# ConvFFN up-projection: the RMSNorm's token factor on the activations instead of on the products

## The chip, the cores and the metric

The kernel runs on one core of a Trainium2 chip. The metric is the device time of one execution in microseconds (us). The core's engines are named as in the profile: PE is TensorE (matmuls; PEld its weight loads), DVE is VectorE, ACT is ScalarE, POOL is GpSimd, and SP (SyncE) issues the weight DMAs. Each engine works off its own queue in order and waits there for the results of the others.

## The reference

Two layers act on x of shape (1, 512, 1024), in float32. Each has a mixer (retention and a state-space scan in layer 0; a convolution module and a complex-diagonal S5 in layer 1), and then a gated ConvFFN, which the change is about:

```python
def rms_norm(x, g, eps=EPS):
    xf = x.astype(F32)
    y = xf * lax.rsqrt(jnp.mean(xf * xf, axis=-1, keepdims=True) + eps)
    return (y * g.astype(F32)).astype(x.dtype)

def conv_ffn(h, w_up, dw_w, dw_b, w_down):
    a = causal_dwconv(h @ w_up, dw_w, dw_b)
    gate, up = jnp.split(a, 2, axis=-1)
    return (jax.nn.silu(gate) * up) @ w_down
...
        f = conv_ffn(rms_norm(x, ffn_norm[i]), ffn_w_up[i], ffn_dw_w[i], ffn_dw_b[i], ffn_w_down[i])
        x = x + f.astype(x.dtype)
```

`w_up` is 1024 x 5632, `w_down` 2816 x 1024. The norm's factor is one number for each token, so it can be applied to the activations ahead of `h @ w_up`, or to the product after it.

## The kernel before

**Tiles.** Channels lie on the 128 partitions and the 512 tokens along the free axis. `x` is eight tiles 128x512. A product in float32 is formed from three matmuls on parts with fewer bits: weights and activations are split into a high part and the rest (`whi`, `wlo`; `xh`, `xl`), and `mm3` adds whi*xh, whi*xl and wlo*xh in PSUM. One *column tile* of the up-projection is 8 channel chunks x 3 = 24 matmuls of 128x512 into one PSUM tile `pup` (four of them). Its weights come by DMA into `wraw` (4 buffers); ACT forms `whi` and DVE `wlo` (3 buffers each, `wload`).

**The norm.** `norm_chunk` splits x*g, without the token factor, into `xh` and `xl` while the layer before still ends. The factor row `R` (128x512, the same on all partitions) is ready only after `norm_end`, which runs behind the first column tile. So `ffn` multiplies each product by `R` when it leaves PSUM (`ffh`, DVE).

**The loop.** `ffn` runs over 22 steps i. Each makes two column tiles, j = i (gate) and j = 22 + i (up); the text numbers these tiles n0 to n43 in the order in which they run. Each tile goes through `ffh` (DVE), the first tap with bias on ACT (`ffa`) and two more taps on DVE (`ffa`, SCALAR_TENSOR_TENSOR). Then ACT's SiLU and DVE's product give `ffg`, which is split into `acth` (ACT) and `actl` (DVE), kept for the down-projection (`pdn`).

**Beside it.** In layer 0, each step takes one piece of a generator, `s5_prep`, which forms the S5 parameters of layer 1. `weights(q)` makes, for four q, `w1r`, `w1i` in six products on POOL (with the scratch `s5t`) and `w2r`, `w2i` in six on DVE (with `s5u`). `store(q)` writes `w2d` and `w1d` by DMAs from POOL; for `w1d`, PE transposes `w1` into PSUM (`pw`) and ACT copies that into `s5t` and `s5u`; four pairs of short matmuls give `pG`. POOL also issues DMAs of a zero tile (`tpd`). Layer 1's ConvFFN has no such work.

**Order.** A scheduler places the instructions of all engines when the program is built, by its own estimates of their times; the order in which an engine's instructions stand is fixed from then on. The code gives only the dependences, the buffers and the order of writing. An instruction added in one place can so move others on every engine.

Of the kernel before, what the change touches and what calls it, by code (L numbers as in the profile page):

```python
# [9 lines left out]
F32 = mybir.dt.float32  # L10
F32R = mybir.dt.float32r
I32 = mybir.dt.int32
AF = mybir.ActivationFunctionType
ALU = mybir.AluOpType
# [5 lines left out]
KC = D // P  # L20
# [5 lines left out]
NPAIR = SH // 2  # L26
POOLTAPS = {0: range(1, 31), 3: range(11, 31)}
WV0 = (0, 1, 3, 6)
PACK0 = (("g_mix0", KC),)
PACK1 = (("ident", P), ("tri", P), ("cw", 48), ("cb", 12), ("dtb", SH), ("alog", SH), ("dsk", NPAIR),  # L30
         ("snw", NPAIR))
# [4 lines left out]
class Trunk:  # L36
    def __init__(self, ctx, tc, ins):
# [14 lines left out]
        self.c = {}  # L52
        self.unpack("c0", PACK0, nc.scalar)
        self.onec = self.const.tile([P, 1], F32, name="onec")
# [1 line left out]
        nc.scalar.activation(self.small("warm", [P, 1], 1), self.onec, AF.Square)  # L56
        self.x = [self.xp.tile([P, T], F32, name=f"x{c}") for c in range(KC)]

    # ---------------------------------------------------------------- helpers
    def unpack(self, name, items, eng):  # L60
        t = self.const.tile([P, sum(n for _, n in items)], F32, name=name)
        eng.dma_start(t, self.ins[name])
        at = 0
        for k, n in items:
            self.c[k] = t[:, at:at + n]
            at += n
# [87 lines left out]
    def norm_chunk(self, st, c, stat=True):  # L154
# [8 lines left out]
        if stat:  # L163
            self.stat_add(st, x)

    def norm_end(self, st):
        st["col"] = self.rstd_cols(st["acc"], D, "rs")
        st["R"] = self.rows(st["col"])

    # ---------------------------------------------------------------- ConvFFN  # L170
    def ffn(self, l, st, nxt, aside=None, out=None):
        nc = self.nc
        ins = self.ins
        dw, db = self.dw[l], self.db[l]
        act = []
        for i in range(NFF):
            ab = []
            for j in (i, NFF + i):
                p = self.pp("pup")
                self.proj(p, ins[f"wup{l}"][j], st["h"])  # L180
                if i == 0 and j == 0:
                    self.norm_end(st)
                h = self.tmp("ffh")
                nc.vector.tensor_tensor(h, p, st["R"], op=ALU.mult)  # L184
                a = self.tmp("ffa")
                nc.scalar.activation(a, h, AF.Identity, scale=dw[:, j, 2:3], bias=db[:, j:j + 1])  # L186
                for tap in (1, 0):
                    s = 2 - tap
                    nc.vector.scalar_tensor_tensor(a[:, s:], h[:, :T - s], dw[:, j, tap:tap + 1], a[:, s:],  # L189
                                                   op0=ALU.mult, op1=ALU.add)  # L190
                ab.append(a)
            if aside is not None:
                next(aside, None)
            gs = self.tmp("ffg")
            nc.scalar.activation(gs, ab[0], AF.Silu)
            nc.vector.tensor_tensor(gs, gs, ab[1], op=ALU.mult)  # L196
            hi, lo = self.slot("acth", F32R), self.slot("actl", F32R)
            self.split(gs, hi, lo)
            act.append((hi, lo))
        nst = self.norm_begin(nxt)  # L200
        spans = [slice(k, min(k + 8, NFF)) for k in range(0, NFF, 8)]
        wdn = lambda c, s: ins[f"wdn{l}"][c, :, s.start * P:s.stop * P]
        for c in range(KC if out is None else KC - 1):
            p = self.pp("pdn")
            for s in spans:
                self.proj(p, wdn(c, s), act[s], start=s.start == 0, stop=s.stop == NFF)
            nc.vector.tensor_tensor(self.x[c], self.x[c], p, op=ALU.add)
            if out is None:
                self.norm_chunk(nst, c)
            else:  # L210
                self.stat_add(nst, self.x[c])
                self.gain(nst, c, slice(0, T))
        if out is None:
            return nst
        # the last channels by halves of the tokens, so that the first half leaves under the second
        c = KC - 1
        w = [self.wload(wdn(c, s), (s.stop - s.start) * P) for s in spans]
        HT = T // 2
        for t in range(2):
            ts = slice(t * HT, (t + 1) * HT)  # L220
            p = self.pp("pdn")[:, :HT]
            for i, s in enumerate(spans):
                self.proj(p, None, [(h[:, ts], lo[:, ts]) for h, lo in act[s]], start=i == 0,
                          stop=s.stop == NFF, w=w[i])
                if t and i == 0:
                    self.finish(nst, 0, out)
            nc.vector.tensor_tensor(self.x[c][:, ts], self.x[c][:, ts], p, op=ALU.add)
        self.finish(nst, 1, out)
# [43 lines left out]
    def load_x(self):  # L272
# [3 lines left out]
        for c in range(KC):  # L276
            nc.sync.dma_start(self.x[c], self.ins["xT"][c])
            self.norm_chunk(st, c, False)
            if c in WV0:
                n = min([k for k in (*WV0, KC) if k > c]) - c  # L280
                hi, lo = self.wload(self.ins["wv0"][:, c * 272:(c + n) * 272], n * 272)
# [3 lines left out]
                self.ident = self.c["ident"]  # L285
        return st

    # ---------------------------------------------------------------- even mixer
    def even(self, st):
        nc = self.nc  # L290
        ins = self.ins
# [7 lines left out]
        def cproj(j, w=None):  # L299
            p = self.pp("pxbc")  # L300
            self.proj(p, ins["wxbc"][j], xs, w=w)
            return p

        # values of the first head and dt, tokens on the partitions
        mm = nc.tensor.matmul
        pv = [self.ps("pv0") for _ in range(NT)]
        for k in range(KC):
            hi, lo = st["w"][k]
# [8 lines left out]
        xd, e, z, z2, q, dt, dA, acs, dec, cdl = [sm("dt" + str(i)) for i in range(10)]  # L317
# [4 lines left out]
        first = [cproj(8), cproj(10)]  # L322
# [2 lines left out]
        self.norm_end(st)  # L325
        R, col = st["R"], st["col"]

        # dt
        bc = lambda t: t.unsqueeze(1).to_broadcast(CH)
        for t in range(NT):  # L330
            nc.vector.scalar_tensor_tensor(xd[:, t, :], xd[:, t, :], col[:, t:t + 1], dtb, op0=ALU.mult, op1=ALU.add)
# [16 lines left out]
        p = self.ps("pacs")  # L348
# [6 lines left out]
        p = self.ps("pacsT")  # L355
# [114 lines left out]
                self.split(y, hi, lo)  # L470
                mix[8 + pr] = (hi, lo)

        # retention
        cosR, sinR = self.slot("cosR"), self.slot("sinR")
        with self.tc.issue_after(self.dma_mark.ins):
            nc.gpsimd.dma_start(cosR, ins["cosT"])
# [131 lines left out]
        self.add_mark = s5_mark  # L608
        return nst

    # ---------------------------------------------------------------- S5 parameters
    def s5_prep(self):
        nc = self.nc
        ins = self.ins
# [5 lines left out]
        def sm(shape=S16):  # L620
            n_[0] += 1
            return self.s5p.tile(shape, F32, name=f"s5_{n_[0]}")
# [6 lines left out]
        with self.tc.issue_after(self.dma_mark.ins), self.tc.issue_after(self.add_mark.ins):  # L629
            lr, li, ls = ld("s5ar", S16), ld("s5ai", S16), ld("s5ls", S16)  # L630
            half = lambda: [t for s_ in [self.slot("s5m")] for t in
                            (s_[:, :256].rearrange("p (a c) -> p a c", c=16),
                             s_[:, 256:].rearrange("p (a c) -> p a c", c=16))]
# [3 lines left out]
            step, x, th, k, m1, m8, s, c, si, co = [sm() for _ in range(10)]  # L637
            magic = 12582912.0
            t, t2_, xc, kk = [sm() for _ in range(4)]
# [38 lines left out]
            den, fr, fi, e = [sm() for _ in range(4)]  # L678
# [22 lines left out]
            def cmul(o_r, o_i, ar, ai, xr, xi, t):  # L701
                tt(o_r, ar, xr, op=ALU.mult)
                tt(t, ai, xi, op=ALU.mult)
                tt(o_r, o_r, t, op=ALU.subtract)
                tt(o_i, ar, xi, op=ALU.mult)
                tt(t, ai, xr, op=ALU.mult)
                tt(o_i, o_i, t, op=ALU.add)
# [7 lines left out]
            S256 = [P, 16, 16]  # L715
            b = lambda t: t.unsqueeze(2).to_broadcast(S256)
            cmul(bbr, bbi, b(fr), b(fi), br, bi, bt)
            # powers by descending exponent: qr[., j] = a^(7-j); the same for a^(8-j)
            pw2_ = self.slot("s5p2")
            qr, qi, wr, wi = [pw2_[:, P * i:P * i + P].rearrange("p (a m) -> p a m", m=8) for i in range(4)]  # L720
            for j in range(8):
# [7 lines left out]
            self.rotd = self.dram.tile([3, 2, P, T], F32, name="rotd")  # L729
            zt = self.slot("s5z")  # L730
            eng.memset(zt, 0.0)
            # chunk rotation e^(i 8 theta k) and the decay |a|^8
            cur = (co, si)
            for n in range(3):
                nx = (sm(), sm())
# [77 lines left out]
            yield  # L813
        toep()

    # ---------------------------------------------------------------- odd mixer
    def odd(self, st):
        nc = self.nc
        ins = self.ins
# [238 lines left out]
        return nst  # L1058


# ---------------------------------------------------------------- host layout
def wtiles(w):
    k, m = w.shape
    return w.reshape(k // P, P, m // P, P).transpose(2, 1, 0, 3).reshape(m // P, P, k)
# [20 lines left out]
def layout(i):  # L1085
# [42 lines left out]
    o["s5dd"] = dd.reshape(P, 512)  # L1128
    for name, items in (("c0", PACK0), ("c1", PACK1), ("c2", PACK2)):
        o[name] = np.concatenate([c[k].reshape(P, -1) for k, _ in items], axis=1)  # L1130
# [28 lines left out]
```

## Time and profile before

| | us |
|---|---|
| median of 3 runs | 1400.68 (1399.62 to 1402.01) |
| span of the profiled execution | 1400.0 |
| PE busy | 1331.6 (95%) |
| DVE busy | 991.1 (71%) |
| ACT busy | 547.9 (39%) |
| POOL busy | 299.2 (21%) |
| up-projection of layer 0 | 412.3 to 678.7 |
| up-projection of layer 1 | 1025.2 to 1266.2 |

The profile takes one execution; all times in rows are us from its start. The span ends 0.7 below the median of the runs. In a row of the timeline, the first number is the start, the second the duration, and a bracket holds the idle time of the engine before it and what ended it. Successive instructions of an engine overlap a little (an end counts the last write), so the cost of one in a full queue is the distance of two starts.

### The profile page before, as it was taken

How to read it: one execution, taken by the hardware profiler on the slowest of the kernel's cores; microseconds unless marked ns; L12 is line 12 of the kernel's file. 1: busy time of each engine (PE TensorE's matmuls, PEld its weight loads, DVE VectorE, ACT ScalarE, POOL GpSimd, SP SyncE). 2: the span in 40 equal slices, each digit the busy share in tenths (PEclk: the TensorE clock that was granted, in tenths of full speed). 3: DMA queues.
4: the chain of work that ended last, by engine and by line, in shares of the span. 5: the costliest groups of instructions: out<-in, count | busy, mean ns of one | idle time of the engine just before them, and what ended most of it. 6: DMA issues, size and time to landing. Idle time of an engine off the chain costs nothing.

```text
span 1400.0 us, 17171 instructions
## 1 busy us (share of the span) xinstructions
PE 1331.6 (95%) x6468; PEld 1104.2 (79%) x6468; DVE 991.1 (71%) x1573; ACT 547.9 (39%) x769; POOL 299.2 (21%) x420
## 2 busy tenths in 40 slices
PE   8999999999999899999999987968799999999997
PEld 7788888888887778888888865756588888888887
DVE  6887777688578998777533369999887777774333
ACT  5455444444353334444322221143444444443221
POOL 0210010002009446800000059769000000000100
PEclk9999999999999999999999997888899999999999
DMA  6432232231244434532333332401142333232321
GB/s 218 153 121 69 75 113 91 90 105 64 90 142 121 124 95 139 177 106 87 98 98 94 106 113 83 143 16 53 62 134 94 103 91 106 90 97 88 102 75 61
DMA packets 48803, 143.00 MB, mean 102 GB/s; under 512 B 6352, under 2 KB 7680, under 8 KB 48720
## 3 DMA queue, kind: packets, MB, share of 16 engines
q1 hardware_dynamic: 42560, 124.34, 28.0%
q0 software_dynamic: 5872, 17.37, 4.3%
q8 instruction: 51, 0.84, 0.2%
q14 instruction: 32, 0.26, 0.1%
q10 hardware_dynamic: 288, 0.19, 0.0%
HBM read 131.88 MB, written 9.99 MB: 101 GB/s over the span
## 4 chain that ended last, share of the span: by engine, by line
PE 78%; DVE 17%; issue 2%; POOL 2%; ACT 1%; DMA 0%; DVEq 0%; ACTq 0%; POOLq 0%
PE pup L101 10%; PE pup L99 10%; PE pup L100 10%; PE pdn L101 6%; PE pdn L99 6%; PE pdn L100 6%; DVE cv L861 3%; DVE wlo L90 3%; PE po L99 2%; PE po L101 2%; PE po L100 2%; DVE ffa L189 1%; PE pxbc L100 1%; PE pxbc L99 1%; PE pxbc L101 1%
## 5 line engine op out<-in xcount | busy, mean ns | idle before, releaser
L89 ACT CAST whi<-wraw 128x1024 fp32r<-128x1024 f32 (+3 forms) x246 | 231.0, 940 | 492.5 <-PE pup L100 131.5
L90 DVE TENSOR_TENSOR wlo<-wraw,whi 128x1024 fp32r<-128x1024 f32 (+3 forms) x242 | 272.7, 1128 | 137.6 <-ACT whi L89 137.5
L101 PE MATMUL pup<-xh,wlo 128*128 128x512 f32 x704 | 276.1, 392 | 9.0 <-DVE wlo L90 9.0
L99 PE MATMUL pup<-xh,whi 128*128 128x512 f32 x704 | 276.5, 393 | 0.0
L100 PE MATMUL pup<-xl,whi 128*128 128x512 f32 x704 | 275.2, 391 | 0.0
L101 PEld LDWEIGHTS pup<-xh,wlo 128*128 128x128 f32 x704 | 133.1, 189 | 38.2 <-DVE wlo L90 10.1
L100 PEld LDWEIGHTS pup<-xl,whi 128*128 128x128 f32 x704 | 133.2, 189 | 27.7
L99 PEld LDWEIGHTS pup<-xh,whi 128*128 128x128 f32 x704 | 133.2, 189 | 27.3
L189 DVE SCALAR_TENSOR_TENSOR ffa<-ffh,c,ffa 128x511 f32<-128x511 f32 (+1 forms) x176 | 149.8, 852 | 2.9
L99 PE MATMUL pdn<-acth,whi 128*128 128x512 f32 (+1 forms) x374 | 140.9, 377 | 0.0
L100 PE MATMUL pdn<-actl,whi 128*128 128x512 f32 (+1 forms) x374 | 140.8, 377 | 0.0
L101 PE MATMUL pdn<-acth,wlo 128*128 128x512 f32 (+1 forms) x374 | 140.8, 377 | 0.0
L184 DVE TENSOR_TENSOR ffh<-pup,R 128x512 f32<-128x512 f32 x88 | 60.5, 687 | 63.6 <-PE pup L101 63.3
L231 POOL TENSOR_SCALAR x<-x,c 128x512 f32<-128x512 f32 (+1 forms) x9 | 9.3, 1034 | 402.0 <-ACT acc L127 302.9
L186 ACT ACTIVATE ffa<-ffh,c 128x512 f32<-128x512 f32 x88 | 71.9, 817 | 49.5 <-DVE ffh L184 47.3
L100 PEld LDWEIGHTS pdn<-actl,whi 128*128 128x128 f32 x374 | 70.4, 188 | 12.9
L101 PEld LDWEIGHTS pdn<-acth,wlo 128*128 128x128 f32 x374 | 70.4, 188 | 12.9
L99 PEld LDWEIGHTS pdn<-acth,whi 128*128 128x128 f32 x374 | 70.4, 188 | 12.8
L100 PE MATMUL po<-ml,whi 128*128 128x512 f32 x192 | 76.5, 399 | 3.8 <-DVE ml L95 3.8
L99 PE MATMUL po<-mh,whi 128*128 128x512 f32 x192 | 76.2, 400 | 0.5 <-ACT mh L94 0.5
L101 PE MATMUL po<-mh,wlo 128*128 128x512 f32 x192 | 76.3, 397 | 0.1
L94 ACT CAST acth<-ffg 128x512 fp32r<-128x512 f32 x44 | 27.3, 621 | 106.7 <-DVE ffg L196 104.4
(424 smaller groups left out, 2436.3 us busy)
## 6 DMA issues: line engine op xcount, KB each, us to landing
wraw<-in_wup_dram SPq DMA_DIRECT2D x88, 512.0 KB, 3.5
wraw<-in_wdn_dram SPq DMA_DIRECT2D x32, 512.0 KB, 3.5
wraw<-in_weo_dram SPq DMA_DIRECT2D x32, 256.0 KB, 3.0
wraw<-in_wxbc_dram SPq DMA_DIRECT2D x12, 512.0 KB, 3.7
wraw<-in_wdn_dram SPq DMA_DIRECT2D x16, 384.0 KB, 3.1
wraw<-in_wz_dram SPq DMA_DIRECT2D x8, 512.0 KB, 3.4
wraw<-in_wg_dram SPq DMA_DIRECT2D x8, 512.0 KB, 3.7
ar<-acd POOLq DMA_DIRECT2D x16, 256.0 KB, 4.0
```

The costliest lines, as they stand in the source:

```text
L89: nc.scalar.copy(hi[:, :n], raw[:, :n])
L90: (eng or nc.vector).tensor_tensor(lo[:, :n], raw[:, :n], hi[:, :n].bitcast(F32), op=ALU.subtract)
L94: self.nc.scalar.copy(hi, src)
L99: mm(out, lhsT=w[0], rhs=x[0], start=start, stop=False)
L100: mm(out, lhsT=w[0], rhs=x[1], start=False, stop=False)
L101: self.mark = mm(out, lhsT=w[1], rhs=x[0], start=False, stop=stop)
L184: nc.vector.tensor_tensor(h, p, st["R"], op=ALU.mult)
L186: nc.scalar.activation(a, h, AF.Identity, scale=dw[:, j, 2:3], bias=db[:, j:j + 1])
L189: nc.vector.scalar_tensor_tensor(a[:, s:], h[:, :T - s], dw[:, j, tap:tap + 1], a[:, s:], op0=ALU.mult, op1=ALU.add)
L231: self.nc.gpsimd.tensor_scalar(self.x[c][:, ts], self.x[c][:, ts], st["g"][:, c:c + 1], 1.0, op0=ALU.mult, op1=ALU.mult)
L861: nc.vector.scalar_tensor_tensor(a[:, s:], cin[i][:, :T - s], kw[:, i, 30 - s:31 - s], a[:, s:], op0=ALU.mult, op1=ALU.add)
```

## The change

`PRE` is 3. In the steps i = 0 and 1, after the aside piece, a new `norm_apply` forms for four channel chunks each `xn` = x*R (DVE), `nh` = its high part with the gain g (ACT) and `nl` = the rest (DVE), into 16 tiles of the pool `slot`, in addition to `xh` and `xl`. From i = 3 on (tiles n6 to n43) the matmuls take `nh`, `nl`; there `ffh` falls away, and ACT's tap and the two DVE taps read PSUM. Tiles n0 to n5 stay as they are. It holds for both layers. (In the diff as written, some comments are dropped too; not shown. Line numbers of the changed kernel are larger: `wlo` L91, matmuls L100 to L102, `xn` L171, `nh` L174, `nl` L175, `ffh` L197, taps L201 and L204, S5 products on POOL L720 to L725, on DVE L791 to L796.)

```diff
+PRE = 3
...
+    def norm_apply(self, st, c):
+        nc = self.nc
+        t = self.tmp("xn")
+        nc.vector.tensor_tensor(t, self.x[c], st["R"], op=ALU.mult)
+        hi, lo = self.slot("nh", F32R), self.slot("nl", F32R)
+        g = st["g"][:, c:c + 1]
+        nc.scalar.activation(hi, t, AF.Copy, scale=g)
+        nc.vector.scalar_tensor_tensor(lo, t, g, hi.bitcast(F32), op0=ALU.mult, op1=ALU.subtract)
+        st.setdefault("hn", []).append((hi, lo))
...
                 p = self.pp("pup")
-                self.proj(p, ins[f"wup{l}"][j], st["h"])
+                self.proj(p, ins[f"wup{l}"][j], st["h"] if i < PRE else st["hn"])
                 if i == 0 and j == 0:
                     self.norm_end(st)
-                h = self.tmp("ffh")
-                nc.vector.tensor_tensor(h, p, st["R"], op=ALU.mult)
+                if i < PRE:
+                    h = self.tmp("ffh")
+                    nc.vector.tensor_tensor(h, p, st["R"], op=ALU.mult)
+                else:
+                    h = p
...
             if aside is not None:
                 next(aside, None)
+            if i < PRE - 1:
+                for c in range(i * KC // (PRE - 1), (i + 1) * KC // (PRE - 1)):
+                    self.norm_apply(st, c)
```

The order moves in both ConvFFNs only. First, DVE in layer 0, before: from the first tap of n0 to the `wlo` of tile n5 (`wlo_4325`); `wlo_4288` is n4's.

```order
L189 SCALAR_TENSOR_TENSOR ffa_3905<-ffh_3903,c2_447,ffa_3905 128x511
L90 TENSOR_TENSOR wlo_4288<-wraw_4286,whi_4287 128x1024
L189 SCALAR_TENSOR_TENSOR ffa_3905<-ffh_3903,c2_447,ffa_3905 128x510
L189 SCALAR_TENSOR_TENSOR ffa_3942<-ffh_3940,c2_447,ffa_3942 128x511
L189 SCALAR_TENSOR_TENSOR ffa_3942<-ffh_3940,c2_447,ffa_3942 128x510
L196 TENSOR_TENSOR ffg_4179<-ffg_4179,ffa_3942 128x512
L184 TENSOR_TENSOR ffh_4217<-pup_4186,R_3901 128x512
L90 TENSOR_TENSOR wlo_4325<-wraw_4323,whi_4324 128x1024
```

After, the same stretch has 39 rows. Its last twelve, up to the `wlo` of n5, which is now `wlo_4373`:

```order
L796 TENSOR_TENSOR w2i_4287<-w2i_4287,s5u_4289 128x512
L171 TENSOR_TENSOR xn_4308<-x5_92,R_3901 128x512
L175 SCALAR_TENSOR_TENSOR nl_4305<-xn_4302,c2_447,nh_4304 128x512
L171 TENSOR_TENSOR xn_4314<-x6_93,R_3901 128x512
L175 SCALAR_TENSOR_TENSOR nl_4311<-xn_4308,c2_447,nh_4310 128x512
L171 TENSOR_TENSOR xn_4320<-x7_94,R_3901 128x512
L175 SCALAR_TENSOR_TENSOR nl_4317<-xn_4314,c2_447,nh_4316 128x512
L214 TENSOR_TENSOR ffg_4326<-ffg_4326,ffa_4280 128x512
L175 SCALAR_TENSOR_TENSOR nl_4323<-xn_4320,c2_447,nh_4322 128x512
L197 TENSOR_TENSOR ffh_4364<-pup_4333,R_3901 128x512
L96 TENSOR_TENSOR actl_4330<-ffg_4326,acth_4329 128x512
L91 TENSOR_TENSOR wlo_4373<-wraw_4371,whi_4372 128x1024
```

Between n4's `wlo` and n5's there stood five instructions; now there are 28, among them seven of the eight `nl`, four `xn`, and the six S5 products `w2` of `weights(0)`, which stood behind n5's `wlo` before.

Second, PE in layer 0 at tile n5, before: each tile is 24 matmuls in a row.

```order
L99 MATMUL pup_4322<-xh_3569,whi_4324 128x512
L100 MATMUL pup_4322<-xl_3570,whi_4324 128x512
L101 MATMUL pup_4322<-xh_3569,wlo_4325 128x512
L99 MATMUL pup_4322<-xh_3595,whi_4324 128x512
L100 MATMUL pup_4322<-xl_3596,whi_4324 128x512
L101 MATMUL pup_4322<-xh_3595,wlo_4325 128x512
```

After, the start of the same tile (`pup_4370`; `pup_4432` is n6, `pup_4467` n7):

```order
L100 MATMUL pup_4370<-xh_3569,whi_4372 128x512
L101 MATMUL pup_4370<-xl_3570,whi_4372 128x512
L100 MATMUL pup_4432<-nh_4181,whi_4434 128x512
L101 MATMUL pup_4432<-nl_4182,whi_4434 128x512
L809 MATMUL pw1_4583<-c1_106,w1r_4284 128x128
L100 MATMUL pup_4467<-nh_4181,whi_4469 128x512
L101 MATMUL pup_4467<-nl_4182,whi_4469 128x512
```

and, after the rest of the first `store`'s short matmuls, the place where the tile goes on:

```order
L816 MATMUL pG_4597<-cdr_4043,w1r_4284 128x32
L817 MATMUL pG_4597<-cdi_4044,w1i_4285 128x32
L809 MATMUL pw1_4783<-c1_106,w1r_4407 128x128
L102 MATMUL pup_4370<-xh_3569,wlo_4373 128x512
L100 MATMUL pup_4370<-xh_3595,whi_4372 128x512
L101 MATMUL pup_4370<-xl_3596,whi_4372 128x512
L102 MATMUL pup_4370<-xh_3595,wlo_4373 128x512
```

The first two matmuls of n5, n6 and n7, the transposes of the first `store` (which before stood behind n9) and one transpose of `w1r_4407`, a result of POOL's `weights(1)`, now stand ahead of the first matmul of n5 that needs `wlo`. In layer 1 the same happens without the S5 work: two matmuls each of n5, n6 and n7, then the rest of n5.

Third, POOL at the same place, before, from the zero tile's DMAs to the second set of products:

```order
L807 DMA tpd_4111<-s5z_4113 640x1x64
L702 TENSOR_TENSOR w1r_4260<-s5p2_4076,s5m_3954 128x512
L703 TENSOR_TENSOR s5t_4264<-s5p2_4076,s5m_3954 128x512
L705 TENSOR_TENSOR w1i_4261<-s5p2_4076,s5m_3954 128x512
L704 TENSOR_TENSOR w1r_4260<-w1r_4260,s5t_4264 128x512
L807 DMA tpd_4111<-s5z_4113 768x1x64
L706 TENSOR_TENSOR s5t_4264<-s5p2_4076,s5m_3954 128x512
L807 DMA tpd_4111<-s5z_4113 896x1x64
L707 TENSOR_TENSOR w1i_4261<-w1i_4261,s5t_4264 128x512
L785 DMA w2d_4110<-w2r_4262 64x4x128 x2
L785 DMA w2d_4110<-w2i_4263 64x4x128 x2
L702 TENSOR_TENSOR w1r_4359<-s5p2_4076,s5m_3954 128x512
```

and after:

```order
L825 DMA tpd_4111<-s5z_4113 896x1x64
L720 TENSOR_TENSOR w1r_4284<-s5p2_4076,s5m_3954 128x512
L721 TENSOR_TENSOR s5t_4288<-s5p2_4076,s5m_3954 128x512
L723 TENSOR_TENSOR w1i_4285<-s5p2_4076,s5m_3954 128x512
L722 TENSOR_TENSOR w1r_4284<-w1r_4284,s5t_4288 128x512
L724 TENSOR_TENSOR s5t_4288<-s5p2_4076,s5m_3954 128x512
L725 TENSOR_TENSOR w1i_4285<-w1i_4285,s5t_4288 128x512
L803 DMA w2d_4110<-w2r_4286 64x4x128 x2
L811 DMA w1d_4109<-s5t_4288 128x512
L803 DMA w2d_4110<-w2i_4287 64x4x128 x2
L811 DMA w1d_4109<-s5u_4289 128x512
L720 TENSOR_TENSOR w1r_4407<-s5p2_4076,s5m_3954 128x512
```

Both last `tpd` DMAs now stand ahead of `weights(0)`, and two DMAs `w1d`, which wait for ACT's copies of the transposes, ahead of `weights(1)`.

## The prediction

> **What bounds the kernel now.** I read the page first, then the stretches of the two ConvFFN up-projections, then single rows there.
>
> ```profile
> span 1400.0 us, 17171 instructions
> PE 1331.6 (95%) x6468; PEld 1104.2 (79%) x6468; DVE 991.1 (71%) x1573; ACT 547.9 (39%) x769; POOL 299.2 (21%) x420
> ...
> PE 78%; DVE 17%; issue 2%; POOL 2%; ACT 1%; DMA 0%; DVEq 0%; ACTq 0%; POOLq 0%
> ...
> L184 DVE TENSOR_TENSOR ffh<-pup,R 128x512 f32<-128x512 f32 x88 | 60.5, 687 | 63.6 <-PE pup L101 63.3
> ```
>
> TensorE (PE) is busy 95% of the span and carries 78% of the chain that ended last. The operation that the change mostly removes, `ffh`, is VectorE (DVE) work, 60.5 us in all, and before it DVE was mostly idle, waiting for PE. So it matters only where DVE makes PE wait. The windows of busy time (start:end, length, then PE, PEld, DVE, ACT and POOL each with its count, granted clock, DMA share, GB/s) show where that is: the up-projection of layer 0 in two parts, and that of layer 1.
>
> ```profile
> 440.00:512.00 72.00, 63.04 (x283) 51.58 (x282) 69.38 (x73) 26.61 (x36) 36.36 (x42) 0.93 0.44 119
> 512.00:678.70 166.70, 166.70 (x761) 138.76 (x760) 129.26 (x159) 71.36 (x91) 60.40 (x104) 1.00 0.40 121
> 1025.22:1266.15 240.93, 240.93 (x1069) 199.46 (x1068) 177.10 (x234) 105.84 (x133) 0.00 (x0) 1.00 0.31 98
> ```
>
> Layer 1, and layer 0 after 512, have PE without a gap: nothing taken from DVE there can shorten them. Only 440 to 512 has a hole, with DVE at 96%. The rows of PE in it (start, duration, engine, line; in brackets idle time and releaser):
>
> ```profile
> 453.09 0.39 PE L100 MATMUL pup<-xl,whi 128*128 128x512 f32 x1
> 459.65 0.80 PE L101 MATMUL pup<-xh,wlo 128*128 128x512 f32 x1 [6.17 <-DVE wlo L90]
> 460.25 0.63 PE L99 MATMUL pup<-xh,whi 128*128 128x512 f32 x1
> 460.68 0.63 PE L100 MATMUL pup<-xl,whi 128*128 128x512 f32 x1
> ...
> 467.11 0.39 PE L99 MATMUL pup<-xh,whi 128*128 128x512 f32 x1
> ...
> 478.21 0.60 PE L791 MATMUL pw<-c,w1r 128*128 128x128 f32 x4
> ...
> 480.79 0.48 PE L99 MATMUL pup<-xh,whi 128*128 128x512 f32 x1
> ...
> 497.24 0.39 PE L99 MATMUL pup<-xh,whi 128*128 128x512 f32 x1
> 497.47 0.39 PE L100 MATMUL pup<-xl,whi 128*128 128x512 f32 x1
> 500.64 0.50 PE L101 MATMUL pup<-xh,wlo 128*128 128x512 f32 x1 [2.79 <-DVE wlo L90]
> ...
> 506.03 0.39 PE L99 MATMUL pup<-xh,whi 128*128 128x512 f32 x1
> ```
>
> Undisturbed matmuls follow each other by 0.2265 us (497.24 to 497.47; 24 in a column tile, 5.44 us). Twice PE waits for `wlo`, the low half of a weight tile: 453.09 to 459.65 loses 6.56 - 0.23 = 6.33 us, 497.47 to 500.64 loses 3.17 - 0.23 = 2.94. After each, matmuls come every 0.43 us for a while (460.25 to 460.68): from 459.65 to 467.11 stand 22 pitches in 7.46 us, 2.48 more than 22 x 0.2265; from 500.64 to 506.03 stand 16 in 5.39, 1.77 more. The two stalls cost 8.81 + 4.71 = 13.5 us. That is the most this change can give back in this window, as I read it.
>
> Numbering column tiles from n0, the tile whose second matmul is the row at 453.09 is n7, and the row at 467.11 begins n8. Now DVE and POOL, which make `wlo` late:
>
> ```profile
> 427.94 1.58 DVE L189 SCALAR_TENSOR_TENSOR ffa<-ffh,c,ffa 128x511 f32<-128x511 f32 x1
> ...
> 432.88 1.51 DVE L196 TENSOR_TENSOR ffg<-ffg,ffa 128x512 f32<-128x512 f32 x1
> ...
> 442.08 1.22 DVE L90 TENSOR_TENSOR wlo<-wraw,whi 128x1024 fp32r<-128x1024 f32 x1
> 443.21 5.01 DVE L189 SCALAR_TENSOR_TENSOR ffa<-ffh,c,ffa 128x511 f32<-128x511 f32 x1
> 448.14 1.86 DVE L777 TENSOR_TENSOR s5u<-s5p,s5m 128x512 f32<-128x512 f32 x1
> 449.93 2.14 DVE L189 SCALAR_TENSOR_TENSOR ffa<-ffh,c,ffa 128x510 f32<-128x510 f32 x1
> ...
> 453.79 5.81 DVE L90 TENSOR_TENSOR wlo<-wraw,whi 128x1024 fp32r<-128x1024 f32 x1
> ...
> 463.27 0.74 DVE L189 SCALAR_TENSOR_TENSOR ffa<-ffh,c,ffa 128x510 f32<-128x510 f32 x1
> 463.94 0.68 DVE L774 TENSOR_TENSOR s5u<-s5p,s5m 128x512 f32<-128x512 f32 x1
> 464.54 0.68 DVE L776 TENSOR_TENSOR w2i<-s5p,s5m 128x512 f32<-128x512 f32 x1
> ```
>
> ```profile
> 440.70 2.63 POOL L807 DMA_DIRECT2D tpd<-s5z  x4 [0.19 <-issue]
> 443.16 1.24 POOL L702 TENSOR_TENSOR w1r<-s5p,s5m 128x512 f32<-128x512 f32 x1
> ...
> 449.94 1.56 POOL L707 TENSOR_TENSOR w1i<-w1i,s5t 128x512 f32<-128x512 f32 x1
> 451.18 1.52 POOL L785 DMA_DIRECT2D w2d<-w2r  x2
> 452.96 1.25 POOL L785 DMA_DIRECT2D w2d<-w2i  x2 [0.27 <-DVE w2i L778]
> 454.22 1.07 POOL L702 TENSOR_TENSOR w1r<-s5p,s5m 128x512 f32<-128x512 f32 x1
> ...
> 457.26 1.25 POOL L704 TENSOR_TENSOR w1r<-w1r,s5t 128x512 f32<-128x512 f32 x1
> ```
>
> DVE's step is 0.67 us for SCALAR_TENSOR_TENSOR (STT: 463.27 to 463.94; I take 0.66), 0.60 for TENSOR_TENSOR (TT) and 1.13 for `wlo` (442.08 to 443.21). While POOL runs its runs of S5 products, DVE instructions of these sorts stretch: 0.74 to 5.01 and 2.14, 0.68 to 1.86, 1.22 to 5.81. The first run, at 443, costs DVE 4.27 + 1.40 + 1.18 = 6.85 us; the first four products of the second, at 454, 4.59. The small ones at 427.94 and 432.88 cost 0.84 + 0.83 = 1.67. Not every instruction stretches:
>
> ```profile
> L837 DVE TENSOR_TENSOR cg<-pcg,R x4: 680/686/692, 817.0 to 919.7; 128x512 f32<-128x512 f32 x4
> ...
> L861 DVE SCALAR_TENSOR_TENSOR cv<-ca,c,cv x60: 710/1053/2706, 829.2 to 984.9; 128x511 f32<-128x511 f32 x2, 128x510 f32<-128x510 f32 x2, 128x509 f32<-128x509 f32 x2, 128x508 f32<-128x508 f32 x2
> ```
>
> In the odd mixer (minimum/median/maximum in ns) the form with one input in PSUM stays within 12 ns, while the form with both in SBUF reaches 2706. The Trainium skill, "SBUF — State Buffer", section "Who interferes with whom", says the same: DVE with two SBUF inputs contends with GpSimd's reads, with at most one it doesn't. By that rule the new `xn` and `nl` (both inputs in SBUF) can be blocked and the later taps, reading `pup`, cannot; the trace agrees as far as it goes.
>
> **The change, part by part.** Removed: 38 `ffh` of each layer, 38 x 0.60 = 22.8 us of DVE. Worth in layer 1 and after 512: nothing, PE covers it. Moved: `ffa` and two taps read PSUM; priced as before, since the PSUM reader `ffh` (687 ns) and SBUF TT (0.68) take the same. The Trainium skill, "Perfetto Trace Analysis", gives a larger access overhead for DVE on PSUM (about 125 ns) than on SBUF (about 60); by it the 76 taps would cost an estimated 76 x 0.065 = 5 us of DVE a layer, which no row here shows. PSUM tiles are held two taps longer, inside the four tiles of slack.
>
> Added per layer: 8 `xn` (0.60), 8 `nl` (0.66) on DVE, 10.1 us, and 8 `nh` on ACT, all within the first two of 22 steps, ahead of the `wlo` of tile n5. The order of the changed kernel shows 39 DVE instructions from the first tap of n0 (row 427.94 before) to the end of n5's `wlo`: 16 STT, 21 TT, 2 `wlo` = 10.56 + 12.6 + 2.26 = 25.4 us; before, there were eight. Also, six S5 products `w2` of the aside work stand ahead of that `wlo`, which before came later.
>
> Layer 0: 427.94 + 25.4 = 453.4. The small blocks add 1.67, the first POOL run 6.85 (the instructions under it now are `w2`, `xn`, `nl`, all SBUF): 461.9. POOL's second run falls in this queue too. POOL now issues two more `tpd` first (2.63/4 = 0.66 each), so its first run starts 1.3 us later; before, those two stood inside that run (443.16 to 451.18), so it still ends at 451.2. Then come six DMA issues in place of four (1.52 + 1.25, and two single ones at 0.66): second run from 455.3, before DVE is through. Its four products block 4.59: n5's `wlo` ends at **466.5**.
>
> PE has its own queue. In the new order, PE takes two matmuls of n5, two each of n6 and n7, then the transposes of S5 weights, and one transpose that needs the fourth product of POOL's second run, and only then n5's `wlo`. That product ends about 455.3 + 3.04 (454.22 to 457.26) + 1.25 = 459.6. So no matter what DVE does, n5 resumes not before 459; by DVE's queue at 466.5. Upper end: the last two products of that run block it too, as the first run's tail did at 449.93 (1.40 and more), about 468.3.
>
> From T = 466.5 PE has 66 matmuls of n5 to n7: 14.95 us, and the half-rate stretch, 2.48 by the stall above, so n8 begins at 483.9, against 467.11: +16.8. The set of transposes (478.21 to 480.79, 2.58) is then done inside the wait: -2.6. The second stall (4.71) should go, since from n6 on a step has 1.2 us less of DVE work and its taps aren't blocked: -4.7. Net **+9.5**; in general T - 457.0.
>
> ```profile
> 1038.48 0.74 DVE L189 SCALAR_TENSOR_TENSOR ffa<-ffh,c,ffa 128x511 f32<-128x511 f32 x1
> ...
> 1053.99 0.39 PE L99 MATMUL pup<-xh,whi 128*128 128x512 f32 x1
> ```
>
> Layer 1: no POOL. From the tap at 1038.48, 27 instructions to n5's `wlo`: 13 x 0.66 + 12 x 0.60 + 2 x 1.13 = 18.0, so 1056.6. PE is at n5 at 1053.99 and has six matmuls (1.36) that don't need `wlo`: 1055.35. Stall 1.2, up to 3.7 if a half-rate stretch as after 459.65 (2.48) follows. I take **+2.1**, nearer the lower end: 1.2 us is less than half of the shorter stall that brought such a stretch (2.79), but eight `nh` now stand between the `whi` on ACT, and `wlo` waits for `whi`.
>
> Sum: 1400.0 + 9.5 + 2.1 = 1411.6. The span of the profiled execution stands 0.7 below the runs' median, 1400.68: forecast **1412**. A measurement tells about 0.2% (2.8 us) from no change.
>
> **Rivals.**
> - *Worse*: the second stall stays, because the backlog (weight tiles n6 and n7 late behind n5) carries through POOL's third run. For it: DVE at 96% before. Against: 1.2 us less per step. Then the sum is T - 452.3, +14 to +16; with layer 1 at 2 to 3.7: 1417 to 1421. Chance 0.22.
> - *Milder*: POOL or DVE meet earlier, PE resumes at 459.6 to 463: +2.6 to +6 in layer 0, about +2 in layer 1, 1405 to 1409. Chance 0.18.
> - *Faster*: the relief wins: the taps on PSUM and the missing `ffh` remove both stalls and the new work hides. At best 1400.7 - 13.5 = 1387; with only the second gone and no new one, 1396, which is what I would expect of it. It decides at T = 454.9 (where +2.1 is cancelled). Against it: DVE needs 453.4 without any block, and PE's queue 459. Only if POOL's first product run started some 5 us earlier would it hold. Chance 0.08.
> - *No change*: the three `wlo` buffers' lead swallows the 10 us. In layer 1 it almost does (1.2 short); in layer 0 not. Chance 0.05.
>
> The forecast's own case has 0.47 (1409 to 1416). Leaving out the faster case and the top of the worse one, the range is 1403 to 1421; faster 0.08, same 0.05, slower 0.87.
>
> **What would show it.** PE without a matmul of `pup` from about 442.5 to 466, released by DVE `wlo` and preceded by `xn`, `nl` on DVE; matmuls every 0.43 us after it; no wait near 497 to 510; in layer 1 one wait of 1 to 2 us near 1055; `ffa` taps on `pup` never over 0.8 us. It is wrong if PE resumes n5 well before 459, if the half-rate stretch after so long an idle time lasts much longer than 2.5 us of loss, or if the taps on PSUM cost more than those on SBUF.

## The result, and the profile after

| | before | after |
|---|---|---|
| median of the runs, us | 1400.49 (1399.62 to 1402.01, 4 runs) | 1412.81 (1412.00 to 1412.98, 4 runs) |
| span of the profiled execution, us | 1400.0 | 1410.9 |
| ratio after/before | | 1.0085, 95% interval 1.0073 to 1.0098 |

The change makes the kernel 0.85% slower (12.3 us between the medians); the forecast was 1412. The profile page of the changed kernel, with the lines that answer to those shown of before, and the taps that now read PSUM:

```profile
span 1410.9 us, 17210 instructions
PE 1328.2 (94%) x6468; PEld 1101.6 (78%) x6468; DVE 953.1 (68%) x1529; ACT 549.7 (39%) x785; POOL 295.6 (21%) x420
...
PE 79%; DVE 15%; POOL 3%; issue 2%; ACT 1%; DMA 0%; DVEq 0%; ACTq 0%; POOLq 0%
...
L204 DVE SCALAR_TENSOR_TENSOR ffa<-pup,c,ffa 128x511 f32<-128x511 f32 (+1 forms) x152 | 113.4, 746 | 2.5
```

DVE has 38 us less to do (953.1 against 991.1) and the kernel is slower: the engine that was relieved is not the one that bounds. Windows of the same stretches, in after's own times (columns as in the prediction):

```profile
440.00:512.00 72.00, 52.33 (x218) 42.85 (x217) 60.41 (x68) 23.62 (x33) 39.23 (x46) 0.81 0.39 105
512.00:689.00 177.00, 177.00 (x818) 147.70 (x817) 115.41 (x139) 73.71 (x99) 53.06 (x106) 1.00 0.40 122
1034.00:1278.00 244.00, 243.09 (x1076) 200.60 (x1075) 162.57 (x214) 107.86 (x143) 0.00 (x0) 1.00 0.32 98
```

PE's hole between 440 and 512 has grown from 9.0 to 19.7 us; elsewhere PE is still full, but for 0.9 us in layer 1. PE waits in layer 0 (line, releaser, us in total, times, longest):

```profile
PE pw L809 <- POOL w1r L722: 14.8, 2, 10.0
PE pup L102 <- DVE wlo L91: 4.3, 1, 4.3
```

and the rows of PE, POOL, ACT and DVE around it, one fence each:

```profile
441.94 0.39 PE L101 MATMUL pup<-nl,whi 128*128 128x512 f32 x1
452.37 0.48 PE L809 MATMUL pw<-c,w1r 128*128 128x128 f32 x1 [10.05 <-POOL w1r L722]
...
463.98 0.47 PE L809 MATMUL pw<-c,w1r 128*128 128x128 f32 x1 [4.76 <-POOL w1r L722]
468.81 0.80 PE L102 MATMUL pup<-xh,wlo 128*128 128x512 f32 x1 [4.35 <-DVE wlo L91]
...
486.18 0.39 PE L100 MATMUL pup<-nh,whi 128*128 128x512 f32 x1
```

```profile
442.14 0.57 POOL L825 DMA_DIRECT2D tpd<-s5z  x1 [0.30 <-POOL s5z L749]
442.92 4.21 POOL L825 DMA_DIRECT2D tpd<-s5z  x6 [0.20 <-issue]
446.77 2.31 POOL L720 TENSOR_TENSOR w1r<-s5p,s5m 128x512 f32<-128x512 f32 x1
...
453.53 1.26 POOL L725 TENSOR_TENSOR w1i<-w1i,s5t 128x512 f32<-128x512 f32 x1
...
462.68 1.25 POOL L722 TENSOR_TENSOR w1r<-w1r,s5t 128x512 f32<-128x512 f32 x1
```

```profile
454.83 0.58 ACT L810 COPY s5t<-pw 128x512 f32<-128x512 f32 x1 [12.54 <-POOL w1i L725]
455.31 0.72 ACT L174 ACTIVATE nh<-xn,c 128x512 fp32r<-128x512 f32 x1
```

```profile
447.48 0.69 DVE L171 TENSOR_TENSOR xn<-x,R 128x512 f32<-128x512 f32 x1
456.07 0.75 DVE L175 SCALAR_TENSOR_TENSOR nl<-xn,c,nh 128x512 fp32r<-128x512 f32 x1 [7.91 <-ACT nh L174]
...
461.73 2.75 DVE L214 TENSOR_TENSOR ffg<-ffg,ffa 128x512 f32<-128x512 f32 x1
...
467.54 1.21 DVE L91 TENSOR_TENSOR wlo<-wraw,whi 128x1024 fp32r<-128x1024 f32 x1
```

These rows form a ring: a chain of waits that begins at POOL, goes through PE's transposes, ACT and DVE, and comes back to PE. PE waits 10 us with a transpose of `w1r`, which POOL ends only at 452. ACT's copy of that transpose stands ahead of `nh` and waits 12.5 us; it starts at 454.83, when POOL's last product of the set, which still reads the scratch `s5t` that the copy overwrites, has ended (453.53 + 1.26). DVE's `nl` waits 7.9 us for `nh`. Behind `nl` stands n5's `wlo`, slowed further by POOL's second set, and for it PE waits last, until 468.81. Tile n8 begins at 486.18, before at 467.11.

The stages, by the first matmuls of `pdn` and of layer 1's `pup` (us; all from the timeline):

| | start of layer 0's `pdn` | from there to layer 1's `pup` | layer 1's up-projection |
|---|---|---|---|
| before | 678.74 | 346.48 | 240.93 |
| after | 690.02 | 344.64 | 242.47 |
| difference | +11.28 | -1.84 | +1.54 |

The sum is +10.98, the spans differ by 10.9. Layer 0's first `pup` matmul stands at 412.29 before and at 411.57 after, so the up-projection of layer 0 itself has grown by 12.0 us. The middle stage is not touched by the edit. In the ten experiments below it lies between 344.25 and 346.59; why it varies is left open.

### The profile page after: what moved, and what is told of

Same layout as the page of the kernel before. It is cut to its first block, busy times and chain, and to the rows that moved or that the text cites. A ratio compares the mean times of both kernels' runs of the same rounds, so it can differ in the third digit from the quotient of the medians.

```text
span 1410.9 us, 17210 instructions
## 1 busy us (share of the span) xinstructions
PE 1328.2 (94%) x6468; PEld 1101.6 (78%) x6468; DVE 953.1 (68%) x1529; ACT 549.7 (39%) x785; POOL 295.6 (21%) x420
## 3 DMA queue, kind: packets, MB, share of 16 engines
q0 software_dynamic: 5872, 17.37, 4.4%
## 4 chain that ended last, share of the span: by engine, by line
PE 79%; DVE 15%; POOL 3%; issue 2%; ACT 1%; DMA 0%; DVEq 0%; ACTq 0%; POOLq 0%
PE pup L102 11%; PE pup L100 10%; PE pup L101 10%; PE pdn L101 6%; PE pdn L102 6%; PE pdn L100 6%; DVE cv L879 4%; PE po L100 2%; PE po L102 2%; PE po L101 2%; DVE wlo L91 2%; PE pxbc L101 1%; PE pxbc L100 1%; PE pxbc L102 1%; PE pyd L471 1%
## 5 line engine op out<-in xcount | busy, mean ns | idle before, releaser
L91 DVE TENSOR_TENSOR wlo<-wraw,whi 128x1024 fp32r<-128x1024 f32 (+3 forms) x242 | 272.3, 1127 | 244.7 <-ACT whi L90 242.0
L100 PE MATMUL pup<-nh,whi 128*128 128x512 f32 x608 | 237.3, 390 | 0.0
L101 PE MATMUL pup<-nl,whi 128*128 128x512 f32 x608 | 236.8, 389 | 0.0
L102 PE MATMUL pup<-nh,wlo 128*128 128x512 f32 x608 | 236.3, 389 | 0.0
L100 PE MATMUL pdn<-acth,whi 128*128 128x512 f32 (+1 forms) x374 | 140.9, 377 | 0.0
L102 PE MATMUL pdn<-acth,wlo 128*128 128x512 f32 (+1 forms) x374 | 140.8, 377 | 0.0
L100 PEld LDWEIGHTS pup<-nh,whi 128*128 128x128 f32 x608 | 114.3, 188 | 24.0 <-ACT whi L90 0.4
L101 PEld LDWEIGHTS pup<-nl,whi 128*128 128x128 f32 x608 | 114.3, 188 | 23.6
L102 PEld LDWEIGHTS pup<-nh,wlo 128*128 128x128 f32 x608 | 114.1, 188 | 23.5
L204 DVE SCALAR_TENSOR_TENSOR ffa<-pup,c,ffa 128x511 f32<-128x511 f32 (+1 forms) x152 | 113.4, 746 | 2.5
L100 PEld LDWEIGHTS pdn<-acth,whi 128*128 128x128 f32 x374 | 70.4, 188 | 13.0
L102 PEld LDWEIGHTS pdn<-acth,wlo 128*128 128x128 f32 x374 | 70.4, 188 | 12.8
L100 PE MATMUL po<-mh,whi 128*128 128x512 f32 x192 | 76.1, 399 | 0.5 <-ACT mh L95 0.5
L102 PE MATMUL po<-mh,wlo 128*128 128x512 f32 x192 | 76.2, 397 | 0.1
L879 DVE SCALAR_TENSOR_TENSOR cv<-ca,c,cv 128x511 f32<-128x511 f32 (+29 forms) x60 | 62.9, 1070 | 1.4 <-ACT cv L860 0.9
L868 POOL TENSOR_SCALAR prod<-cp,c 128x512 f32<-128x512 f32 x50 | 54.2, 1084 | 30.2 <-DVE cp L857 25.7
```

The costliest lines, as they stand in the source:

```text
L91: (eng or nc.vector).tensor_tensor(lo[:, :n], raw[:, :n], hi[:, :n].bitcast(F32), op=ALU.subtract)
L100: mm(out, lhsT=w[0], rhs=x[0], start=start, stop=False)
L101: mm(out, lhsT=w[0], rhs=x[1], start=False, stop=False)
L102: self.mark = mm(out, lhsT=w[1], rhs=x[0], start=False, stop=stop)
L868: nc.gpsimd.tensor_scalar(t, a, kw[:, i, 30 - s:31 - s], 1.0, op0=ALU.mult, op1=ALU.mult)
L879: nc.vector.scalar_tensor_tensor(a[:, s:], cin[i][:, :T - s], kw[:, i, 30 - s:31 - s], a[:, s:], op0=ALU.mult, op1=ALU.add)
```

## The experiments

**Each layer alone.** `PRE` holds in one layer only:

```diff
-                self.proj(p, ins[f"wup{l}"][j], st["h"] if i < PRE else st["hn"])
+                self.proj(p, ins[f"wup{l}"][j], st["h"] if i < PRE or l != 0 else st["hn"])
```

(likewise for `ffh` and `norm_apply`; `l != 1` in the second run).

> The change in layer 0 alone; layer 1 as before. If the loss sits in layer 0, as the traces suggest (first down-projection matmul 11.3 us later there, 1.8 us given back in the odd mixer, 1.5 us lost again in layer 1), this is 1.5 to 2 us faster than the full change: about 1411, ratio 1.0075. Rival, the loss is shared by both layers alike: about 1406.5.

> The change in layer 1 alone; layer 0 as before. Loss in layer 0: about 1402, ratio 1.001, with one wait of PE for wlo of 1 to 2 us after n5's first two matmuls. Loss shared alike: about 1406.5.

Measured: layer 0 alone 1411.82 us, ratio to the kernel before 1.0076 (1.0063 to 1.0090); layer 1 alone 1401.49, ratio 1.0006 (0.9997 to 1.0014), where before had 1400.97. In time, layer 1's part can't be told from nothing, but the stage shows it: 242.44 us with the change in layer 1, 240.94 without. The loss sits in layer 0.

**The removal alone.** The projection keeps `st["h"]` and `norm_apply` isn't called, so from n6 on the token factor is left out:

```diff
-                self.proj(p, ins[f"wup{l}"][j], st["h"] if i < PRE else st["hn"])
+                self.proj(p, ins[f"wup{l}"][j], st["h"])
...
-            if i < PRE - 1:
+            if False:
```

> Only the removal: from the seventh column tile on ffh is left out and ACT and the taps read PSUM, nothing is formed in advance (the token factor is missing from these tiles). The prediction's term: the stall near 497 goes and the one near 453 stays, because it lies ahead of the seventh tile's outputs: -4.7 us, 1396. Rival A, the removal is worth nothing, since POOL's products cause both stalls: 1400.5. Rival B, both stalls go: 1387.

Measured: 1395.17 us, ratio 0.9959 (0.9944 to 0.9974): -5.8. One wait of PE for `wlo` is left in layer 0, 6.1 us; before had two, 9.0 in all. The removal by itself takes away the second stall and no more: the up-projection of layer 0 is 261.64 us long, 4.8 less than before's 266.45. The rest of the gain lies in the middle stage (344.91 against 346.48), which the edit doesn't touch.

**The addition alone.** `xn`, `nh`, `nl` are formed and not used; `ffh` stays everywhere.

```diff
-                self.proj(p, ins[f"wup{l}"][j], st["h"] if i < PRE else st["hn"])
+                self.proj(p, ins[f"wup{l}"][j], st["h"])
...
-                if i < PRE:
+                if True:
```

> Only the addition: xn, nh, nl are formed in steps 0 and 1 of both layers, but all column tiles go on with xh, xl and ffh as before. Theory: the addition makes the wait at n5 by itself, and the removal takes away the second stall (the run with the removal alone gained 5.8 us): the full change plus 4.7 to 5.8 us, about 1418. Rival: the second stall was tied to the first and goes with it whatever is removed: as the full change, 1412.

Measured: 1412.91 us, ratio 1.0090 (1.0073 to 1.0107), as the full change. My theory gave 1418 and falls: the second stall is gone here too, although all `ffh` are back. So in the full change the missing `ffh` buys nothing that can be measured (the up-projection of layer 0 takes 278.15 us here, 278.45 in after). A row of after shows why: POOL's third run still blocks a `wlo`,

```profile
477.26 5.68 DVE L91 TENSOR_TENSOR wlo<-wraw,whi 128x1024 fp32r<-128x1024 f32 x1 [0.17 <-ACT whi L90]
```

but it ends near 483, and PE, late by its long wait, comes to the tile at 486.18. The 4.5 us of blocking lie under a backlog of PE's own making.

**Is it the ring?** The full change, with the short matmuls of `store` held in PE's order until the step's last column matmul:

```diff
+                with self.tc.issue_after(self.mark.ins):
+                    for i in range(4):
...
+                        nc.tensor.transpose(p[:, s], w[:, s], self.ident)
```

(and the same around the two `pG` matmuls). ACT's copies then stand behind `nh`.

> The full change, but the transposes and short matmuls of store are held in PE's order until the step's last column matmul, so that ACT's copies stand behind nh. Theory 1, the loss in layer 0 is the chain POOL products - PE transposes - ACT copies - nh - nl - wlo: without it DVE reaches n5's wlo by its own volume, at 455 to 462 in place of 468.7, and the time falls by 6 to 10 us, to 1403 to 1407. Theory 2, as forecast: DVE's volume with POOL's blocks sets it, and the chain only stands where those blocks would: wlo again at 466 to 468, and 1411 to 1414.

Measured: 1413.63 us, ratio 1.0089 (1.0076 to 1.0103). PE's waits and, of DVE and POOL, the rows in which they meet:

```profile
PE pup L102 <- DVE wlo L91: 22.1, 1, 22.1
```

```profile
448.52 1.54 DVE L175 SCALAR_TENSOR_TENSOR nl<-xn,c,nh 128x512 fp32r<-128x512 f32 x1
449.98 1.54 DVE L171 TENSOR_TENSOR xn<-x,R 128x512 f32<-128x512 f32 x1
451.44 1.54 DVE L175 SCALAR_TENSOR_TENSOR nl<-xn,c,nh 128x512 fp32r<-128x512 f32 x1
...
459.76 2.64 DVE L96 TENSOR_TENSOR actl<-ffg,acth 128x512 fp32r<-128x512 f32 x1
462.32 3.29 DVE L91 TENSOR_TENSOR wlo<-wraw,whi 128x1024 fp32r<-128x1024 f32 x1
```

```profile
449.48 1.49 POOL L721 TENSOR_TENSOR s5t<-s5p,s5m 128x512 f32<-128x512 f32 x1
450.93 1.50 POOL L723 TENSOR_TENSOR w1i<-s5p,s5m 128x512 f32<-128x512 f32 x1
```

The ring is gone: DVE no longer waits for `nh`, PE for no transpose. In its place POOL's first set, in turn with `nl` and `xn`, stretches DVE's queue by 6.2 us (448.52 to 459.16, for instructions whose steps make 4.44), where it idled 7.9 before. PE resumes at 465.67 (466.5 in the forecast, 468.81 in after). The two bounds, the ring in after and DVE's queue here, lie within 3.2 us of each other, so taking the ring away can gain no more than that. And even that isn't kept: n8 begins at 483.33, 2.85 us earlier than in after, but the first set of transposes, which in after stands inside the wait, now takes 2.58 us of PE's time at 494.21. So the time is the same.

**The S5 work later.** The generator of the aside work gets four empty pieces ahead of its first:

```diff
-        for f, q in ((weights, 0), (weights, 1), (nop, 0), (store, 0), (weights, 2), (store, 1), (weights, 3), (store, 2),
+        for f, q in ((nop, 0), (nop, 0), (nop, 0), (nop, 0), (weights, 0), (weights, 1), (nop, 0), (store, 0), (weights, 2), (store, 1), (weights, 3), (store, 2),
```

> The full change with the aside work (the S5 parameters) begun four steps later. POOL's products then run beside the taps that read PSUM, and n5's wlo has 27 DVE instructions ahead and in it, as in layer 1: 427.3 + 18.0 + 1.4 of small blocks = 446.8, against PE's arrival at 442.6. A stall of 3 to 4.5 us, with up to 2.5 of half rate after it, and none later: before less 13.5, plus 3 to 7, plus 1.5 in layer 1: 1392 to 1396. If POOL's products weren't the larger part of the loss: 1405 or more.

Measured: 1402.60 us, ratio 1.0012 (1.0003 to 1.0022), 10 us better than the change and 6.6 over the upper end of the range of 1392 to 1396. n5's `wlo` comes as worked out (PE resumes at 447.50 after 3.16 us of waiting), but POOL, which has nothing else to do, starts its first products at 447.97 all the same: the scheduler moved DVE's `w2` products (to 488), the transposes (to 526) and POOL's later sets (to 496) back, but not POOL's first six products. These fall on `nl`, and PE waits again at n7:

```profile
447.36 5.87 DVE L175 SCALAR_TENSOR_TENSOR nl<-xn,c,nh 128x512 fp32r<-128x512 f32 x1
```

```profile
459.42 0.79 PE L102 MATMUL pup<-nh,wlo 128*128 128x512 f32 x1 [5.23 <-DVE wlo L91]
```

Two more runs, both with the four empty pieces, tried to keep POOL's first products out of there. The first put `issue_after` around them:

```diff
+            with self.tc.issue_after(self.mark.ins):
+                cmul(v(w1r), v(w1i), pw(qr), pw(qi), mt(bbr), mt(bbi), v(t1))
```

> As the full change with the aside work four steps later, but POOL's products of each weights piece are also held until the step's last column matmul, so that the first set can't run beside nl, ffg and wlo of tiles n5 to n7. If POOL's products blocking DVE are what is left of the loss there (nl 5.87 us in place of 0.74, then 5.23 us of waiting at n7), that wait goes and only the one at n5 (3.2 us and some half rate) stays, with layer 1's 1.5: 1387.7 + 4 to 5.5 + 1.5 = 1393 to 1395. If it is DVE's own volume: 1401 to 1403 again.

Measured: 1401.84 us, ratio 1.0009 (0.9999 to 1.0018). It answers nothing: the products still began at 447.32. `issue_after` only sets an order for the scheduler: here POOL didn't wait for the matmul named. The second, without `issue_after`, made a true dependence, a one-column read of a late `acth` on POOL:

```diff
+            if q == 0:
+                eng.tensor_scalar(sm([P, 1]), self.late[:, :1].bitcast(F32), 0.0, 1.0, op0=ALU.mult, op1=ALU.mult)
             cmul(v(w1r), v(w1i), pw(qr), pw(qi), mt(bbr), mt(bbi), v(t1))
...
             act.append((hi, lo))
+            self.late = hi
```

> As the run before, where POOL's first products still started at 447 (the hold set only their place in the queue): now one tiny POOL instruction ahead of them reads acth of the fourth step, so that they can't start before tile n7 is through. Same question. POOL's products blocking DVE make the wait at n7: it goes, only n5's wait (3.2 us and some half rate) and layer 1's 1.5 stay, 1393 to 1395. DVE's own volume makes it: 1401 to 1403. Third case, the block only moves with the products and makes another wlo late some 4 us after they start: 1397 to 1400.

Measured: 1398.92 us, ratio 0.9989 (0.9979 to 0.9998): the third case. The products start at 480.79, the wait at n7 is gone, and there is a new one of 2.54 us, with a half-rate stretch behind it. The `wlo` that PE waits for there is not itself stretched (1.21 us); it stands in DVE's queue behind `w2` products, some of them held up by POOL's second set:

```profile
496.21 2.80 DVE L794 TENSOR_TENSOR w2r<-s5p,s5m 128x512 f32<-128x512 f32 x1
...
503.95 1.21 DVE L91 TENSOR_TENSOR wlo<-wraw,whi 128x1024 fp32r<-128x1024 f32 x1
```

```profile
505.22 0.79 PE L102 MATMUL pup<-nh,wlo 128*128 128x512 f32 x1 [2.54 <-DVE wlo L91]
```

So the wait at n7 did come from POOL's products; holding them gains 3.7 us against the run with the S5 work later (3.4 in the up-projection of layer 0), and the rest of that loss turns up at another tile. How much of the new wait is POOL's blocking and how much the time of the `w2` products themselves isn't separated.

**Away from the crowded steps.** The kernel before, with eight empty pieces ahead of the aside work and no other edit; and the change with `PRE = 6` (chunks spread over five steps) and four empty pieces.

> The kernel before with the aside work begun eight steps later, and no other edit. If both stalls of before come from S5 products meeting the DVE backlog at the start of the up-projection (the norm's rows, the last xl, the first R), they go: 1400.7 - 13.5 = 1387. Rival: POOL's products block DVE wherever they stand, and the stalls only move: 1400.

> The full change with PRE = 6 (the eight chunks formed over five steps, tiles from n12 on without ffh) and the aside work begun four steps later. If PE is the bound once the collision is gone, the missing ffh adds nothing on top: the same as the kernel before with the aside eight steps later, 1387 to 1389. If DVE's relief is worth something of its own: below 1385.

Measured: 1387.70 us, ratio 0.9906 (0.9891 to 0.9921), and 1387.74, ratio 0.9906 (0.9891 to 0.9920). The window of the kernel before with the eight empty pieces:

```profile
440.00:512.00 72.00, 72.00 (x320) 59.60 (x319) 59.06 (x68) 31.17 (x39) 13.04 (x15) 1.00 0.38 116
```

PE is full there, and DVE at 82% in place of 96%. Both versions beat the kernel before by 13 us, close to the most that the prediction had named as available in the two stalls (13.5). But POOL's first set has not left these steps, and still holds DVE up, by 6 us over two taps:

```profile
445.81 1.45 POOL L702 TENSOR_TENSOR w1r<-s5p,s5m 128x512 f32<-128x512 f32 x1
```

```profile
444.97 7.57 DVE L189 SCALAR_TENSOR_TENSOR ffa<-ffh,c,ffa 128x511 f32<-128x511 f32 x2
```

What has gone from there is the rest: DVE's `w2` products, the transposes with ACT's copies, and POOL's second set, which in before ran at 454 and held up a `wlo` and now runs at 527. With that much less in its queue DVE makes up for the block, and PE doesn't wait at all. Which of the three parts matters most was not tested. With PE full (but for one wait of 1.19 us in the version with `PRE = 6`), the missing `ffh` of 32 tiles a layer adds nothing: PE is the bound.

## Why the prediction was right, and where not

- *Which resource, which tiles.* Right. The loss is at n5 of layer 0, by a late `wlo`; nothing is gained where PE was full.
- *When PE resumes.* 466.5 against 468.81. The time was close, the account of it was not: I let DVE's queue set it, with 6.85 us of blocking by POOL's first run. In after, DVE was not blocked in that run; it idled 7.9 us for `nh` behind ACT's copy, which stands ahead of `nh` in ACT's queue, and I didn't follow that queue. That 7.9 and 6.85 are so close is luck. The second run did block DVE, as forecast: from 456.07 to 468.67 ten instructions take 12.6 us where their steps make 6.8, 5.8 more (4.59 forecast). I had followed PE's own wait for POOL, but only as a lower bound (459); I also had all transposes behind n7's two matmuls, where one stands ahead of them, which changes no term. The run with the transposes held shows the account of the forecast as it would have stood without the ring: 465.67, with 6.2 us of blocking by the first run and about 4.1 by the second.
- *POOL's start.* Mis-sized: I took two more DMA issues, 1.3 us, and began the first run at 444.4; it began at 446.77. The first `tpd` was already late, 442.14 against 439.93, because POOL's small copies ahead of it meet `xn`, `nl` and the taps on a DVE that no longer pauses (rows in the last section). The ring begins at POOL's first run, so a late start moves all of it; 2.2 us is about what PE's resumption was off by (2.3), but no run tests that link.
- *From there to n8.* 66 matmuls and the half-rate stretch: 17.43 in the forecast, 486.18 - 468.81 = 17.37 measured, 2.42 of it for the half rate (2.48 forecast). The forecast had assumed that a wait three times as long has no longer stretch behind it, and it had none.
- *The set of transposes, -2.6, and the second stall, -4.7.* Both came off: +19.07 - 2.58 - 4.71 = 11.8, against +11.28 measured (12.0 counted from the stage's own start). But the reason that I gave for the second, the missing `ffh` and the unblocked taps, is refuted by the run with the addition alone: the stall goes with PE's delay. The missing `ffh` removes it only where there is no such delay.
- *Layer 1.* +2.1 forecast, +1.54 measured, of which the row shows 0.90 as PE waiting for `wlo`. The 1.2 from the instruction count was nearer than what I added to it for a half-rate stretch: there was none.

```profile
1066.16 0.50 PE L102 MATMUL pup<-xh,wlo 128*128 128x512 f32 x1 [0.90 <-DVE wlo L91]
```

- *The sum.* Layer 0 came out 1.8 us worse than forecast (11.28 against 9.5), layer 1 0.6 better, and the middle stage, for which the forecast had no term, gave 1.84 back. That the total was met within 1 us is in part luck; without the middle stage it would have been about 1414.6, still inside the range.

- *Taps on PSUM.* Priced as before, right: 746 ns on average over 152, and no blocking. The list of that line in after (minimum/median/maximum in ns):

```profile
L204 DVE SCALAR_TENSOR_TENSOR ffa<-pup,c,ffa x152: 736/745/751, 488.3 to 1279.6; 128x511 f32<-128x511 f32 x76, 128x510 f32<-128x510 f32 x76
```

  In after, POOL's products hardly meet one of them. In the run with the products after n7 they do, a product and a tap on `pup` at the same time, right behind a product of DVE with both inputs in SBUF that stretched (1.54 where 0.68 is usual):

```profile
500.00 1.62 POOL L726 TENSOR_TENSOR w1i<-w1i,s5t 128x512 f32<-128x512 f32 x1
```

```profile
498.93 1.54 DVE L795 TENSOR_TENSOR s5u<-s5p,s5m 128x512 f32<-128x512 f32 x1
500.39 0.73 DVE L204 SCALAR_TENSOR_TENSOR ffa<-pup,c,ffa 128x511 f32<-128x511 f32 x1
```

  So the rule of the Trainium skill ("SBUF — State Buffer", "Who interferes with whom") holds in this case for one input in PSUM and one in SBUF. The larger overhead on PSUM that the Trainium skill gives ("Perfetto Trace Analysis", "Optimizing Scalar/DVE Operations") isn't to be seen here: the taps on SBUF in layer 1 of before took 745 and 750 ns.

- *The rival that ended faster* needed both stalls to go. They can (1387.7), but by moving S5 work out of these steps and not by leaving out `ffh`.

## What to carry to other kernels

Work taken from an engine that isn't the bound pays only where that engine makes the bound wait; look for those places first, and ask whether the total or the crowd at one moment makes them. Here it was the crowd: a one-time preparation put into the two most crowded steps cost 12 us, and moving most of the other one-time work out of those steps gained 13. A block of 6 us that stayed there cost nothing once the queue behind it was short enough. When an edit lets the scheduler reorder, follow each waiting instruction through every queue that it now stands ahead of; a copy on a quiet engine can hold up two busy ones.

## What the runs showed of the hardware

DVE and POOL hold each other up in two ways. A DVE instruction with both inputs in SBUF that is running or starting when a set of POOL products begins can be held until the fourth of them is over (5.01 us in before, 5.87 in the run with the S5 work later, where 0.74 is usual; 5.81 and 5.68 for `wlo`, where 1.22 is usual), while POOL goes on at about 1.03 us each. These four end about 0.55 us (the two of 0.74) and 1.09 us (the two `wlo`) after POOL's fourth product, not much less than their steps of 0.66 and 1.13, as if they got to work only then. The first four products overlap one another, and the first pause between two products comes after the fourth (0.08 us in after, 481.85 to 481.93). That this pause lets DVE in is an inference, which no run tests. Or the two take turns: in the run with the transposes held, `nl` and `xn` followed each other every 1.46 us, and so did POOL's products, both slowed. What decides between the two ways is open. I had priced only the first. POOL loses by it too. In after, one of its smallest copies, 128x16, took 3.66 us beside three `xn` and a `wlo` in a row, and others 0.7, where 0.20 is usual:

```profile
430.74 0.70 POOL L740 COPY s5p<-s5p 128x16 f32<-128x16 f32 x1
431.39 3.66 POOL L741 COPY s5p<-s5p 128x16 f32<-128x16 f32 x1
435.00 0.20 POOL L742 COPY s5p<-s5p 128x16 f32<-128x16 f32 x1
```

PE's half-rate stretch hardly grew with the idle time ahead of it: 2.48 us lost after 6.17 us of waiting in before, 2.42 in after, after a wait from 442 to 469 with little but short matmuls in it, and 2.71 after 22.14 us without any matmul in the run with the transposes held. After shorter waits it is smaller (1.77 after 2.79 us, in before), and after the 0.90 us in layer 1 there was none.
